# Two sums of weights per chunk by adding transfers, and a new route for turned blocks, in a hybrid transformer block on one core

## The chip, the cores and the metric

The kernel runs on one core of a Trainium2 chip. The metric is the device time of one launch in microseconds. The engines that matter are PE (matrix products, its weight loads shown as PEld), DVE and ACT (elementwise work), POOL and SP, which here do little but issue transfers: SP the loads of the weights, POOL the transfers of turned blocks. PE's clock has two levels, 2.4 and 1.2 GHz; the profile shows the granted one as a share of the higher.

## What is computed

One decoder layer on 256 tokens of 2048 values, in fp32. Cut to what matters:

```python
h = rmsnorm(x, attn_norm_w)
q, k, v, o, ig, fg, dq, dk, dv, gm, gd = split_in(h @ w_in)
hm = sigmoid(o) * head_rmsnorm(mlstm_chunkwise(q, k, v, ig, fg))
hd = head_rmsnorm(diff_attention(dq, dk, dv, lam)) * (1 - lam_init)
y  = sigmoid(gm) * (hm @ w_bm) + sigmoid(gd) * (hd @ w_bd)
x  = x + y @ w_out                                   # product wo
h  = rmsnorm(x, ffn_norm_w)
x  = x + (silu(h @ w_gate) * (h @ w_up)) @ w_down    # products fgu, fd; inner width 5632
return rmsnorm(x, final_norm_w)
```

## The kernel before

**Products.** Every weight is read from DRAM by SP in pieces of 1 MB (tiles `wr_...`, four buffers) and split into a high part (`wh`, a copy on ACT, L337) and a low part (`wl`, a subtraction on DVE, L341), so that three fp32r matmuls (L180, L181, L182: high by high, low by high, high by low) give the accuracy of fp32. The split of half a piece is a unit. It is made four units before PE uses it, into five buffers, so the copy of a unit waits until PE is through with the unit five before.

**Pairs.** The feed-forward part is a row of products: `fgu0` to `fgu3`, `fd00`, `fd02`, `fgu4` to `fgu7`, `fd10`, `fd12`, `fgu8` to `fgu10`, `fd20`, `fd22`, and `fd23`. All but the last two are pairs (16 of them), each of two blocks of 512 columns over four chunks of 512 rows (three in `fd20`). A pair takes one chunk by a scheme of seven products in place of eight (table SEVEN), in which some operands are sums: sums of blocks of x (made once per chunk by `add_up`, L160 to L164), and sums of weights, four per pair, each an addition in place on DVE (L329). The first chunk's seven units are dealt evenly among the plain units of the others. At a pair's end eight differences and sums on DVE (L416, tiles `q`) take its results from PSUM; for `fgu` an ACT Silu (L1123) and a DVE multiply (L1125) of each token half then make a block `g` of the inner layer. This happens while PE is already in the next pair.

**Turned blocks.** PE wants the left operand with its features in the partitions. A block of 256 tokens by 512 features gets there in one of three ways. `turn_task` has DVE turn it in squares of 32 (two transposes, L261), sends it to DRAM (one transfer from POOL's queue, L266), reads it back in another order (four, L271), and copies it into a high and a low part (L284 and L285, or with a scale L288 to L290); between the steps stand waits counted in ticks of the program's order, 4 and 10, one tick being six matmuls, so the place of a step in each engine's queue is fixed when the program is written. `turn_short_task` does it with 16 transposes of DVE (L230) and no DRAM. `transpose_task` uses eight transposes on PE (L193). The sets TURN and SHORT say which block takes which way. The blocks are y0 to y3 (input of `wo`), x1_0 to x1_3 (input of `fgu`; the last is `x1last`), g (input of `fd`; the last is `glast`), and some before. Lanes (`side.push("tr", ...)`) hold tasks that run one after the other: a block in a lane starts when the one ahead of it is through.

**Order.** Every engine executes its instructions in the order in which this program wrote them; an instruction that waits holds up all behind it on its engine.

Of the kernel before, what the change touches and what calls it, by code (L numbers as in the profile page):

```python
# [50 lines left out]
def hybrid_block(ctx, tc, x, attn_norm_w, w_in, conv_w, conv_b, b_igate, b_fgate, mlstm_norm_w,  # L51
# [266 lines left out]
    class Op:


        def __init__(self, pair, chunk, raw, half, add, uses, frees):
            self.pair, self.chunk, self.raw, self.half, self.add = pair, chunk, raw, half, add
            self.uses, self.frees, self.added, self.parts = uses, frees, False, None

        def sum_up(self):

            if self.add and not self.added:
                o, x = (feed.raw[g][:, 2 * h:2 * h + 2] for g, h in ((self.raw, self.half), self.add))
                nc.vector.tensor_tensor(out=o, in0=o, in1=x, op=ALU.add)  # L329
            self.added = True  # L330
# [990 lines left out]
```

## Time and profile before

| | |
|---|---|
| time, median of 3 runs | 1784.65 us (1783.57 to 1785.12) |
| the profiled execution | 1783.87 us, of which the span is 1781.8 us |
| mean granted clock of PE in it | 0.988 |
| PE / PEld / DVE / ACT / POOL busy | 97 / 80 / 71 / 52 / 5 % |
| DMA traffic | 362.52 MB, mean 203 GB/s |
| units split in pairs, `fgu` / `fd` | 209 / 91 |
| additions of weights on DVE (L329) | 64 of 1.22 us |

Busy is the time in which an engine executed something. A row of the timeline gives start and length in microseconds, engine, line, operation, output and inputs, and in brackets how long the engine was idle before it and which engine's instruction ended that. A table of waits sums these idle times by what waited and by what was waited for. Matmuls overlap in the pipeline: one lasts 0.39 us by its row and the next starts 0.23 us after it at the full clock; at half the clock the rows show 0.63 and 0.43 us.

### The profile page before, as it was taken

To read this page: it belongs to the slowest core of one execution; us is meant where nothing else is said; L and a number is where in the kernel's file an instruction comes from. 1 tells how busy PE (TensorE), PEld (TensorE's weight loads), DVE (VectorE), ACT (ScalarE), POOL (GpSimd) and SP (SyncE) were. 2 spreads that over 40 slices of the span, in tenths; PEclk is the share of its full clock that TensorE was granted. 3 is DMA by queue.
4 is the path that set the end of the run, shared out by engine and by line. 5 is a ranking of instruction groups with operands and counts; after the bars stand their busy time and mean duration, and the time that the engine had idled before them with its cause. 6 is when DMAs were issued, how large, how long until landed. Compare 5 with 4: busy or idle time off the path is not lost.

```text
span 1781.8 us, 20497 instructions
## 1 busy us (share of the span) xinstructions
PE 1735.7 (97%) x7769; PEld 1431.4 (80%) x7769; DVE 1272.4 (71%) x1692; ACT 921.1 (52%) x1189; POOL 86.0 (5%) x176
## 2 busy tenths in 40 slices
PE   9999999999999999999998988999999999999987
PEld 7888888888888888888887866788788787788766
DVE  6776876655456667665565666888788888788886
ACT  7555655654345555565443544555444555445543
POOL 1000000000001000100001000000000000000000
PEclk9999999999999999999999988999999999999999
DMA  9656566665677766766675745676566666566643
GB/s 305 198 167 185 167 200 177 190 230 200 189 217 216 215 203 189 210 191 211 230 243 195 227 144 171 202 243 223 188 205 219 206 235 229 179 205 226 219 171 116
DMA packets 179619, 362.52 MB, mean 203 GB/s; under 512 B 9904, under 2 KB 11584, under 8 KB 179520
## 3 DMA queue, kind: packets, MB, share of 16 engines
q1 hardware_dynamic: 169744, 330.78, 57.8%
q0 software_dynamic: 9744, 30.42, 5.7%
q8 instruction: 61, 1.00, 0.2%
q14 instruction: 38, 0.31, 0.0%
q10 hardware_dynamic: 32, 0.01, 0.0%
HBM read 343.88 MB, written 17.30 MB: 203 GB/s over the span
## 4 chain that ended last, share of the span: by engine, by line
PE 91%; DVE 4%; DMA 2%; issue 2%; ACT 2%; POOL 0%; SPq 0%; ACTq 0%; DVEq 0%; POOLq 0%
PE acc_fgu_P L181 7%; PE acc_fgu_P L180 7%; PE acc_fgu_P L182 7%; PE acc_fd_P L180 4%; PE acc_fd_P L182 4%; PE acc_fd_P L181 4%; PE acc_mo L180 2%; PE acc_mv L180 2%; PE acc_gm L180 2%; PE acc_dk L180 2%; PE acc_dq L180 2%; PE acc_gd L180 2%; PE acc_dv L182 2%; PE acc_dv L180 2%; PE acc_gd L182 2%; PE acc_mo L182 2%
## 5 line engine op out<-in xcount | busy, mean ns | idle before, releaser
L341 DVE TENSOR_TENSOR wl_fgu<-wr_fgu,wh_fgu 128x1024 fp32r<-128x1024 f32 x209 | 252.5, 1221 | 78.1 <-ACT wh_fgu L337 73.6
L337 ACT CAST wh_fgu<-wr_fgu 128x1024 fp32r<-128x1024 f32 x209 | 214.9, 1050 | 180.3 <-PE acc_fgu_P L182 107.6
L180 PE MATMUL acc_fgu_P<-wh_fgu,x1Th 128*128 128x512 f32 x594 | 234.0, 394 | 15.4 <-ACT x1Th L289 13.3
L181 PE MATMUL acc_fgu_P<-wl_fgu,x1Th 128*128 128x512 f32 x594 | 234.0, 394 | 4.1 <-DVE wl_fgu L341 4.1
L182 PE MATMUL acc_fgu_P<-wh_fgu,x1Tl 128*128 128x512 f32 x594 | 233.4, 393 | 0.0
L180 PEld LDWEIGHTS acc_fgu_P<-wh_fgu,x1Th 128*128 128x128 f32 x594 | 113.0, 190 | 40.3 <-ACT x1Th L289 14.1
L337 ACT CAST wh_fd<-wr_fd 128x1024 fp32r<-128x1024 f32 x91 | 94.0, 1050 | 91.2 <-PE acc_fd_P L182 67.4
L341 DVE TENSOR_TENSOR wl_fd<-wr_fd,wh_fd 128x1024 fp32r<-128x1024 f32 x91 | 110.2, 1222 | 38.9 <-ACT wh_fd L337 37.4
L181 PEld LDWEIGHTS acc_fgu_P<-wl_fgu,x1Th 128*128 128x128 f32 x594 | 112.9, 190 | 28.8 <-DVE wl_fgu L341 5.3
L182 PEld LDWEIGHTS acc_fgu_P<-wh_fgu,x1Tl 128*128 128x128 f32 x594 | 113.0, 190 | 23.8 <-DVE x1Tl L290 0.5
L266 POOL DMA_DIRECT2D across<-turned x29 | 16.4, 565 | 1421.5 <-DVE turned L261 1421.5
L271 POOL DMA_DIRECT2D across<-across x116 | 63.2, 552 | 144.2 <-DMA across<-turned 62.3
L485 DVE TENSOR_TENSOR wl_bm<-wr_bm,wh_bm 128x1024 fp32r<-128x1024 f32 x32 | 39.2, 1225 | 40.5 <-ACT wh_bm L484 40.5
L485 DVE TENSOR_TENSOR wl_dv<-wr_dv,wh_dv 128x1024 fp32r<-128x1024 f32 x32 | 39.2, 1224 | 37.0 <-ACT wh_dv L484 37.0
L485 DVE TENSOR_TENSOR wl_bd<-wr_bd,wh_bd 128x1024 fp32r<-128x1024 f32 x32 | 39.2, 1225 | 34.1 <-ACT wh_bd L484 34.1
L485 DVE TENSOR_TENSOR wl_wo<-wr_wo,wh_wo 128x1024 fp32r<-128x1024 f32 x32 | 38.9, 1222 | 33.2 <-ACT wh_wo L484 33.2
L485 DVE TENSOR_TENSOR wl_dk<-wr_dk,wh_dk 128x1024 fp32r<-128x1024 f32 x32 | 39.2, 1224 | 28.7 <-ACT wh_dk L484 28.7
L485 DVE TENSOR_TENSOR wl_gm<-wr_gm,wh_gm 128x1024 fp32r<-128x1024 f32 x32 | 39.1, 1224 | 27.9 <-ACT wh_gm L484 27.7
L485 DVE TENSOR_TENSOR wl_dq<-wr_dq,wh_dq 128x1024 fp32r<-128x1024 f32 x32 | 39.1, 1222 | 27.4 <-ACT wh_dq L484 27.3
L485 DVE TENSOR_TENSOR wl_gd<-wr_gd,wh_gd 128x1024 fp32r<-128x1024 f32 x32 | 39.1, 1223 | 26.9 <-ACT wh_gd L484 26.9
L484 ACT CAST wh_bd<-wr_bd 128x1024 fp32r<-128x1024 f32 x32 | 33.7, 1054 | 47.2 <-PE acc_bd L182 40.5
L484 ACT CAST wh_bm<-wr_bm 128x1024 fp32r<-128x1024 f32 x32 | 33.7, 1054 | 46.7 <-PE acc_bm L182 39.9
(430 smaller groups left out, 4635.9 us busy)
## 6 DMA issues: line engine op xcount, KB each, us to landing
wr_fgu<-in_w_ffn_gate_dram SPq DMA_DIRECT2D x44, 1024.0 KB, 5.2
wr_fgu<-in_w_ffn_up_dram SPq DMA_DIRECT2D x44, 1024.0 KB, 5.1
wr_fd<-in_w_ffn_down_dram SPq DMA_DIRECT2D x44, 1024.0 KB, 5.1
wr_mo<-in_w_in_dram SPq DMA_DIRECT2D x16, 1024.0 KB, 5.4
wr_mv<-in_w_in_dram SPq DMA_DIRECT2D x16, 1024.0 KB, 5.4
wr_gm<-in_w_in_dram SPq DMA_DIRECT2D x16, 1024.0 KB, 5.7
wr_bm<-in_w_branch_m_dram SPq DMA_DIRECT2D x16, 1024.0 KB, 5.1
wr_dq<-in_w_in_dram SPq DMA_DIRECT2D x16, 1024.0 KB, 5.4
```

What stands on the lines that cost most here:

```text
L180: nc.tensor.matmul(o, lhsT=a[0], rhs=b[0], start=first, stop=False)
L181: nc.tensor.matmul(o, lhsT=a[0], rhs=b[1], start=False, stop=False)
L182: nc.tensor.matmul(o, lhsT=a[1], rhs=b[0], start=False, stop=last)
L266: nc.gpsimd.dma_start(out=d.rearrange("a f b n -> (a f) (b n)"), in_=y.rearrange("p b k t s -> p (b k t s)"))
L271: nc.gpsimd.dma_start(out=t[32 * b:32 * b + 32].rearrange("p a u s -> p a (u s)"), in_=d[:, :, b].rearrange("a f n -> f a n"))
L337: nc.scalar.copy(out=hi, in_=r)
L341: nc.vector.tensor_tensor(out=lo, in0=r, in1=hi.bitcast(F32), op=ALU.subtract)
L484: nc.scalar.copy(out=hi[:, i:i + step], in_=r)
L485: nc.vector.tensor_tensor(out=lo[:, i:i + step], in0=r, in1=hi[:, i:i + step].bitcast(F32), op=ALU.subtract)
```

## The change

Four edits. (1) The table SEVEN gets a new order of units (P3, P2, P1, P4 to P7), and each unit a list of the sums that are formed after its split. Two, both after P2's split, stay additions on DVE; the other two, after P1's and P4's split, become transfers from SBUF to SBUF that add to their destination, issued from POOL's queue, 512 KB each. (2) `side.across` starts a turned block at once when its kind is in TURN and not in SHORT, in place of putting it in a lane. (3) SHORT holds `x1last` in place of `glast`; `glast`, which is in neither set then, goes through PE. (4) The Silu and the multiply that make `g` are written one tick later.

```diff
-SHORT = {"glast"}
+SHORT = {"x1last"}
...
+        def across(self, lane, kind, *rest):
+
+            gen = across_task(kind, *rest)
+            if kind in TURN and kind not in SHORT:
+                self.spawn(gen)
+            else:
+                self.push(lane, gen)
...
-    SEVEN = (("P3", (0, 1), None, (0, 1)), ("P1", (0, 0), None, (0, 0)), ("P2", (1, 0), None, "d"),
-             ("P4", (1, 0), (1, 1), "a"), ("P5", (1, 1), (0, 1), "b"), ("P6", (0, 1), (1, 0), "c"),
-             ("P7", (0, 0), (0, 1), (1, 0)))
+    VEC, DMA = "vector", "transfer"
+    SEVEN = (("P3", (0, 1), (0, 1), ()),
+             ("P2", (1, 0), "d", ((VEC, (1, 0), (1, 1)), (VEC, (1, 1), (0, 1)))),
+             ("P1", (0, 0), (0, 0), ((DMA, (0, 1), (1, 0)),)),
+             ("P4", (1, 0), "a", ((DMA, (0, 0), (0, 1)),)),
+             ("P5", (1, 1), "b", ()), ("P6", (0, 1), "c", ()), ("P7", (0, 0), (1, 0), ()))
...
-            self.sum_up()
...
-            nxt = feed.units[feed.nsplit + 1:feed.nsplit + 2]
-            if nxt and isinstance(nxt[0], Op):
-                nxt[0].sum_up()
             nc.vector.tensor_tensor(out=lo, in0=r, in1=hi.bitcast(F32), op=ALU.subtract)
+            for how, *terms in self.sums:
+                o, x = (feed.raw[g][:, 2 * h:2 * h + 2] for g, h in terms)
+                if how == VEC:
+                    nc.vector.tensor_tensor(out=o, in0=o, in1=x, op=ALU.add)
+                else:
+                    nc.gpsimd.dma_start(out=o, in_=x, accum_op=ALU.add)
...
-            side.push("tr", across_task("y" if c < 3 else "ylast", s, yT, c, None, 2 if c < 3 else 4))
+            side.across("tr", "y" if c < 3 else "ylast", s, yT, c, None, 2 if c < 3 else 4)
...
-            side.push("tr", across_task("x1" if c < 3 else "x1last", t, x1T, c, ffn_col, 2 if c < 3 else 4))
+            side.across("tr", "x1" if c < 3 else "x1last", t, x1T, c, ffn_col, 2 if c < 3 else 4)
...
                 t, c, q = got
+                yield
                 if c == 0:
                     nc.scalar.activation(out=g[:, t], in_=q, func=AF.Silu, scale=r2(t))
...
-            side.push("tr", across_task("g" if i < 2 or len(gT.hi) > 3 else "glast", g, gT, i, None, 4))
+            side.across("tr", "g" if i < 2 or len(gT.hi) > 3 else "glast", g, gT, i, None, 4)
```

Line numbers of the kernel after are some eight to ten higher (L261 becomes L269, L329 becomes L346, L341 becomes L342, L1125 becomes L1135). POOL's queue gets 32 adding transfers, from `fgu0` to `fd20`; in a pair whose predecessor gave a block `g`, the second one stands between that block's way out and its way back.

How the instructions move, at three places. First DVE around the start of `wo`; `sgd_6954` is the block y2 before, made in `bd2`, `sgd_7105` is y3, made in `bd3`, and `turned` is a block's first transposes. Before, y2 is turned behind the instructions that make y3:

```order
L485 TENSOR_TENSOR wl_wo_7686<-wr_wo_7599,wh_wo_7685 128x1024
L285 TENSOR_TENSOR yTl_7682<-across,yTh_7681 128x512
L485 TENSOR_TENSOR wl_wo_7704<-wr_wo_7599,wh_wo_7703 128x1024
L1084 TENSOR_TENSOR sgd_7105<-acc_bd_0_7572,sgd_7105 128x512
L1085 TENSOR_TENSOR sgd_7105<-y_3395,sgd_7105 128x512
L1084 TENSOR_TENSOR sgd_7105<-acc_bd_1_7573,sgd_7105 128x512
L1085 TENSOR_TENSOR sgd_7105<-y_3395,sgd_7105 128x512
L485 TENSOR_TENSOR wl_wo_7730<-wr_wo_7633,wh_wo_7729 128x1024
L261 STREAM_TRANSPOSE turned<-sgd_6954 128x4x4x32 x2
```

In the change (y2 is `sgd_6959`):

```order
L1093 TENSOR_TENSOR sgd_6959<-acc_bd_0_7417,sgd_6959 128x512
L1094 TENSOR_TENSOR sgd_6959<-y_3244,sgd_6959 128x512
L1093 TENSOR_TENSOR sgd_6959<-acc_bd_1_7418,sgd_6959 128x512
L1094 TENSOR_TENSOR sgd_6959<-y_3244,sgd_6959 128x512
L494 TENSOR_TENSOR wl_bd_7580<-wr_bd_7484,wh_bd_7579 128x1024
L494 TENSOR_TENSOR wl_bd_7596<-wr_bd_7484,wh_bd_7595 128x1024
L269 STREAM_TRANSPOSE turned<-sgd_6959 128x4x4x32 x2
```

The transposes of y2 stand two splits behind the instructions that make it, in `bd3`'s splits, in place of after the first ones of `wo`.

Second, DVE at the start of `fgu0`; `x_3` is the last block of x1, `x_2` the one before. Before:

```order
L1097 TENSOR_TENSOR x_3_7725<-acc_wo_1_8223,x_3_7725 128x512
L341 TENSOR_TENSOR wl_fgu_8387<-wr_fgu_8249,wh_fgu_8386 128x1024
L261 STREAM_TRANSPOSE turned<-x_2_7570 128x4x4x32
L341 TENSOR_TENSOR wl_fgu_8408<-wr_fgu_8285,wh_fgu_8407 128x1024
L261 STREAM_TRANSPOSE turned<-x_2_7570 128x4x4x32
L341 TENSOR_TENSOR wl_fgu_8422<-wr_fgu_8337,wh_fgu_8421 128x1024
L341 TENSOR_TENSOR wl_fgu_8445<-wr_fgu_8411,wh_fgu_8444 128x1024
L329 TENSOR_TENSOR wr_fgu_8337<-wr_fgu_8337 128x1024
L341 TENSOR_TENSOR wl_fgu_8467<-wr_fgu_8411,wh_fgu_8466 128x1024
L341 TENSOR_TENSOR wl_fgu_8480<-wr_fgu_8337,wh_fgu_8479 128x1024
```

In the change:

```order
L1106 TENSOR_TENSOR x_3_7735<-acc_wo_1_8228,x_3_7735 128x512
L342 TENSOR_TENSOR wl_fgu_8397<-wr_fgu_8358,wh_fgu_8396 128x1024
L346 TENSOR_TENSOR wr_fgu_8358<-wr_fgu_8358 128x1024
L346 TENSOR_TENSOR wr_fgu_8358<-wr_fgu_8358,wr_fgu_8249 128x1024
L342 TENSOR_TENSOR wl_fgu_8418<-wr_fgu_8301,wh_fgu_8417 128x1024
L238 STREAM_TRANSPOSE turned<-x_3_7735 32x2x4x32 x4
L342 TENSOR_TENSOR wl_fgu_8436<-wr_fgu_8249,wh_fgu_8435 128x1024
L238 STREAM_TRANSPOSE turned<-x_3_7735 32x2x4x32 x4
L298 TENSOR_TENSOR x1Tl_8462<-scaled,x1Th_8461 128x512
L238 STREAM_TRANSPOSE turned<-x_3_7735 32x2x4x32 x4
L342 TENSOR_TENSOR wl_fgu_8473<-wr_fgu_8421,wh_fgu_8472 128x1024
L298 TENSOR_TENSOR x1Tl_8462<-scaled,x1Th_8461 128x512
```

The two long transposes of `x_2` are gone from here (they stand in `wo`), sixteen short ones of `x_3` have come in, as four times four rows, and two additions (L346) stand in a row behind one split.

Third, DVE at the end of `fgu1`, in `fgu2`'s first units; `wl_fgu_9027` before is the first unit's low part, `wl_fgu_9095` the fifth's, `wl_fgu_9118` the sixth's; the `q` are the results of `fgu1`. Before:

```order
L341 TENSOR_TENSOR wl_fgu_9047<-wr_fgu_8984,wh_fgu_9046 128x1024
L416 TENSOR_TENSOR q_8809<-acc_fgu_P_8765,q_8809 128x512
L341 TENSOR_TENSOR wl_fgu_9065<-wr_fgu_8954,wh_fgu_9064 128x1024
L341 TENSOR_TENSOR wl_fgu_9077<-wr_fgu_9008,wh_fgu_9076 128x1024
L416 TENSOR_TENSOR q_8811<-acc_fgu_P_8769,q_8811 128x512
L341 TENSOR_TENSOR wl_fgu_9095<-wr_fgu_8984,wh_fgu_9094 128x1024
L416 TENSOR_TENSOR q_8810<-acc_fgu_P_8825,q_8810 128x512
L1125 SCALAR_TENSOR_TENSOR g<-q_8810,rs_x_8523,g 128x512
L416 TENSOR_TENSOR q_8812<-acc_fgu_P_8829,q_8812 128x512
L1125 SCALAR_TENSOR_TENSOR g<-q_8812,rs_x_8523,g 128x512
L341 TENSOR_TENSOR wl_fgu_9118<-wr_fgu_9008,wh_fgu_9117 128x1024
```

In the change (the fifth unit is `wl_fgu_9101`, the sixth `wl_fgu_9124`):

```order
L425 TENSOR_TENSOR q_8816<-acc_fgu_P_8773,q_8816 128x512
L342 TENSOR_TENSOR wl_fgu_9071<-wr_fgu_8961,wh_fgu_9070 128x1024
L342 TENSOR_TENSOR wl_fgu_9083<-wr_fgu_9008,wh_fgu_9082 128x1024
L425 TENSOR_TENSOR q_8818<-acc_fgu_P_8777,q_8818 128x512
L342 TENSOR_TENSOR wl_fgu_9101<-wr_fgu_9074,wh_fgu_9100 128x1024
L346 TENSOR_TENSOR wr_fgu_9074<-wr_fgu_9074 128x1024
L346 TENSOR_TENSOR wr_fgu_9074<-wr_fgu_9074,wr_fgu_8990 128x1024
L425 TENSOR_TENSOR q_8817<-acc_fgu_P_8831,q_8817 128x512
L1135 SCALAR_TENSOR_TENSOR g<-q_8817,rs_x_8564,g 128x512
L425 TENSOR_TENSOR q_8819<-acc_fgu_P_8835,q_8819 128x512
L342 TENSOR_TENSOR wl_fgu_9124<-wr_fgu_9008,wh_fgu_9123 128x1024
L1135 SCALAR_TENSOR_TENSOR g<-q_8819,rs_x_8564,g 128x512
```

Two additions have come in between the fifth and the sixth split, and the second multiply that makes `g` has gone behind the sixth. The four sums of block `gT0` (L160 to L164 before), which stood ahead of the first unit's split, now stand some rows further up, between the second and the third `q` row.

## Rows read from the trace of the kernel before

**Rows 1.** Page, busy time of each engine: microseconds, share, instructions.

```profile
PE 1735.7 (97%) x7769; PEld 1431.4 (80%) x7769; DVE 1272.4 (71%) x1692; ACT 921.1 (52%) x1189; POOL 86.0 (5%) x176
```

**Rows 2.** Waits of PE: total microseconds, times, longest.

```profile
PE acc_fgu_P L180 <- ACT x1Th L289: 13.3, 2, 7.4
PE acc_wo L180 <- ACT yTh L284: 5.3, 1, 5.3
PE acc_fd_P L180 <- ACT gT2h L241: 5.2, 1, 5.2
PE acc_fgu_P L181 <- DVE wl_fgu L341: 4.1, 3, 1.4
```

**Rows 3.** Timeline, PE around `wo` chunk 2: start, duration; idle before, releaser.

```profile
951.13 0.79 PE L180 MATMUL acc_wo<-wh_wo,yTh 128*128 128x512 f32 x1 [5.34 <-ACT yTh L284]
...
955.01 0.40 PE L180 MATMUL acc_wo<-wh_wo,yTh 128*128 128x512 f32 x1
```

**Rows 4.** Timeline, DVE and ACT around `wo`, block y2.

```profile
938.25 1.30 DVE L261 STREAM_TRANSPOSE turned<-sgd 128x512 f32<-128x512 f32 x2
...
950.46 1.14 ACT L284 CAST yTh<-across 128x512 fp32r<-128x512 f32 x2 [3.59 <-DMA across<-across]
```

**Rows 5.** Timeline, PE at the start of `fgu0`.

```profile
1033.13 0.57 PE L180 MATMUL acc_fgu_P<-wh_fgu,x1Th 128*128 128x512 f32 x1 [2.14 <-DVE x L1097]
...
1055.82 0.79 PE L180 MATMUL acc_fgu_P<-wh_fgu,x1Th 128*128 128x512 f32 x1 [5.88 <-ACT x1Th L289]
...
1060.68 0.39 PE L182 MATMUL acc_fgu_P<-wh_fgu,x1Tl 128*128 128x512 f32 x1
```

**Rows 6.** Line L329, instructions of DVE: count, durations in ns.

```profile
L329 DVE TENSOR_TENSOR wr_fgu<-wr_fgu x22: 1211/1218/1221, 1044.0 to 1684.9; 128x1024 f32<-128x1024 f32 x22
```

**Rows 7.** Timeline, DVE, then PE, around the end of `fgu1`.

```profile
1131.97 1.23 DVE L164 TENSOR_TENSOR gT0sl<-sums,gT0sh 128x1024 fp32r<-128x1024 f32 x1 [1.12 <-ACT gT0sh L163]
...
1149.05 1.22 DVE L341 TENSOR_TENSOR wl_fgu<-wr_fgu,wh_fgu 128x1024 fp32r<-128x1024 f32 x1
...
1150.32 0.50 PE L181 MATMUL acc_fgu_P<-wl_fgu,x1Th 128*128 128x512 f32 x1 [1.36 <-DVE wl_fgu L341]
```

**Rows 8.** Timeline, DVE, then PE, behind the end of `fgu2`.

```profile
1187.92 0.68 DVE L416 TENSOR_TENSOR q<-acc_fgu_P,q 128x512 f32<-128x512 f32 x1
1188.64 0.75 DVE L1125 SCALAR_TENSOR_TENSOR g<-q,rs_x,g 128x512 f32<-128x512 f32 x1
1189.31 1.22 DVE L341 TENSOR_TENSOR wl_fgu<-wr_fgu,wh_fgu 128x1024 fp32r<-128x1024 f32 x1
...
1192.66 0.39 PE L181 MATMUL acc_fgu_P<-wl_fgu,x1Th 128*128 128x512 f32 x1
```

**Rows 9.** Timeline, POOL, then ACT, in `fd00`.

```profile
1243.00 1.10 POOL L271 DMA_DIRECT2D across<-across  x2 [2.37 <-issue]
...
1253.77 0.61 ACT L284 CAST gT0h<-across 128x512 fp32r<-128x512 f32 x1
```

**Rows 10.** Timeline, DVE, then PE, in `fd20`.

```profile
1707.00 0.75 DVE L1125 SCALAR_TENSOR_TENSOR g<-q,rs_x,g 128x512 f32<-128x512 f32 x1
1711.20 0.87 DVE L230 STREAM_TRANSPOSE turned<-g 32x256 f32<-32x256 f32 x2
...
1722.74 0.79 PE L180 MATMUL acc_fd_P<-wh_fd,gT2h 128*128 128x512 f32 x1 [5.24 <-ACT gT2h L241]
...
1726.30 0.39 PE L182 MATMUL acc_fd_P<-wh_fd,gT2l 128*128 128x512 f32 x1
```

**Rows 11.** Line L193, transposes on PE of one block in `wo`.

```profile
L193 PE MATMUL ps_tr<-ident,sgd x8: 270/272/273, 958.4 to 959.2; 128*128 128x128 f32 x8
```

**Rows 12.** Line L266: from issue to landing.

```profile
DMA to landing us min/median/max: 3.3/4.9/7.6
```

**Rows 13.** Page, DMA queues: packets, MB, share of 16 engines.

```profile
q0 software_dynamic: 9744, 30.42, 5.7%
```

**Rows 14.** Windows, the pair product `fgu3`.

```profile
1181.00:1223.00 42.00, 42.00 (x187) 34.78 (x186) 35.73 (x38) 22.09 (x25) 2.74 (x5) 1.00 0.67 225
```

More of the change, by code (lines that the diff above doesn't have):

```diff
@@ L311, in __init__ @@
             self.hooks, self.ahead, self.by_token, self.steps = {}, AHEAD, False, {}
-    SEVEN = (("P3", (0, 1), None, (0, 1)), ("P1", (0, 0), None, (0, 0)), ("P2", (1, 0), None, "d"),
-             ("P4", (1, 0), (1, 1), "a"), ("P5", (1, 1), (0, 1), "b"), ("P6", (0, 1), (1, 0), "c"),
-             ("P7", (0, 0), (0, 1), (1, 0)))
-    class Op:
[L321 to L330, printed above, removed]
+    VEC, DMA = "vector", "transfer"
[4 more added lines that the diff above has]
+             ("P5", (1, 1), "b", ()), ("P6", (0, 1), "c", ()), ("P7", (0, 0), (1, 0), ()))
+    class Op:
+        def __init__(self, pair, chunk, raw, half, uses, sums, frees):
+            self.pair, self.chunk, self.raw, self.half = pair, chunk, raw, half
+            self.uses, self.sums, self.frees, self.parts = uses, sums, frees, None
         def split(self):
-            self.sum_up()
             r = feed.raw[self.raw][:, 2 * self.half:2 * self.half + 2]
@@ L360, in plan @@
                 if ch in self.sums:
-                    for i, (bank_, (blk, h), add, x) in enumerate(SEVEN):
+                    for i, (bank_, (blk, h), x, sums) in enumerate(SEVEN):
                         frees = [(ch, 1)] if i == 5 else [(ch, 0)] if i == 6 else []
-                        sevens.append((ch, (ch, blk), h, add and ((ch, add[0]), add[1]), [(bank_, x)], frees))
+                        sums = [(how, *(((ch, b), h2) for b, h2 in terms)) for how, *terms in sums]
+                        sevens.append((ch, (ch, blk), h, [(bank_, x)], sums, frees))
                 else:
@@ L367, in plan @@
                             uses = [((("P1", "P7"), ("P2", "P8"))[blk][t], (t, h)) for t in range(TT)]
-                            plain.append((ch, (ch, blk), h, None, uses, [(ch, blk)] if h else []))
+                            plain.append((ch, (ch, blk), h, uses, [], [(ch, blk)] if h else []))
             order = sorted([((i + 0.5) / len(l), n, x) for n, l in enumerate((sevens, plain)) for i, x in enumerate(l)],
@@ L373, in plan @@
             self.ops = []
-            for ch, raw, h, add, uses, frees in order:
+            for ch, raw, h, uses, sums, frees in order:
                 if raw not in keys:
@@ L377, in plan @@
                     feed.groups.append((self, raw))
-                self.ops.append(Op(self, ch, keys[raw], h, add and (keys[add[0]], add[1]), uses,
-                                   [keys[f] for f in frees]))
+                self.ops.append((ch, raw, h, uses, sums, frees))
+            self.ops = [Op(self, ch, keys[raw], h, uses, [(how, *((keys[r], h2) for r, h2 in terms)) for how, *terms in sums],
+                           [keys[f] for f in frees]) for ch, raw, h, uses, sums, frees in self.ops]
             feed.units += self.ops
@@ L1061, in f @@
             qk[side_name] = dst
-            side.push("conv", across_task("d" + side_name, tok, dst, 0, rate=2))
+            side.across("conv", "d" + side_name, tok, dst, 0)
         return f
```

4 lines of the change are left out of this document (2 added, 2 removed).

## The prediction

> **What bounds the kernel now.** I read the busy times first: PE works 97% of the span, DVE 71% [rows 1]. With PE that full, only two things can shorten the time: fewer matmuls (the change leaves their number as it is, but for eight transposes) or fewer holes in PE. So the second view was the table of PE's waits. Its large entries are few [rows 2]: 13.3 us at two blocks of x1, 5.3 at a block of y, 5.2 at the last g, and 4.1 in three waits for a low part of weights. Third, I followed each into the timeline, where a hole costs more than its length. Behind the wait for y2, 5.34 us long, the matmuls from 951.13 to 955.01 are nine in 3.88 us [rows 3]; in a full stretch a matmul takes 42.00/187 = 0.225 us [rows 14], nine 2.03. The start at half clock costs 1.85 us more. So does the one behind x1's third block: eleven matmuls from 1055.82 to 1060.68 in 4.86 us in place of 2.48, 2.4 more [rows 5]. Fourth, the windows: in `fgu3` PE is busy without a break while DVE is busy 35.73 and ACT 22.09 of 42.00 us [rows 14]. There, work taken from DVE is worth nothing by itself. What decides is the work that stands in front of a low part that PE is about to need.
>
> **The change part by part.**
>
> *Block y2.* It is turned at 938.25, and ACT's copy waits at 950.46 for the last of its transfers [rows 4]: 12.2 us from the one to the other. In the new order its transposes stand two splits behind the instructions that make it, in `bd3`, about 24 us earlier by the place in the program. The copy is then ready long before. I take off 5.34 + 1.85 = **-7.2**; the bounds are 0 and -7.2, since nothing larger hangs on it.
>
> *Blocks 2 and 3 of x1.* Before: holes of 2.14, 5.88 and 7.41 us [rows 2, 5], 15.4 in all, with 2.4 us of half clock behind each of the two long ones and some 1.7 behind the short one (an estimate: it was shorter), so 21.9. The 2.14 waits for DVE's addition that frees a bank and stays, with its 1.7. Block 2 is turned in `wo`, so its hole goes. Block 3 no longer goes through DRAM but by sixteen transposes on DVE, 0.87/2 = 0.44 us each by the rows of `glast` [rows 10], 7.0 us, between splits and beside two additions of 1.22 [rows 6]. Following DVE's new order, the last transpose is through about 17.7 us into `fgu0`, and the copies of the turned block, on ACT, stand ahead of the copy of unit 8. PE reaches unit 8 after 78 matmuls, 17.6 us in. I put 2.7 us of new holes at units 8 to 10, and 0.8 of half clock. Before 21.9, after 2.14 + 1.7 + 2.7 + 0.8 = 7.4: **-14.5**. Bounds: -18 (no new holes) and -8 (the new ones are a whole DVE queue late, about as long as one old hole).
>
> *Ends of `fgu1`, `fgu5`, `fgu9`.* PE waits there 4.1 us in three waits [rows 2]: the sixth unit's low part starts at 1149.05 and lasts 1.22, and PE goes on at 1150.32 [rows 7]. In front of it DVE now has two additions more (2.44) and one multiply less (0.75): 1.7 us later. Besides, the sums of block g, whose last part starts at 1131.97 after 1.12 us of waiting and takes 1.23 [rows 7], now stand behind the first unit's split and not ahead of it; DVE makes up some of these 2.35 us in its pauses, and I take 1.3 of them. So +3.0 at each of three places, **+9**; from 1.7 to 4.1 each, 5 to 12.
>
> *The other seven ends of `fgu` products that give a turned g.* The sixth unit's part starts at 1189.31, ends at about 1190.5, and PE uses it at 1192.66 [rows 8]: 2.1 us to spare. The same 1.7 us fit, with 0.4 left: **0**. This is the cover that is nearly gone. Each microsecond beyond costs seven.
>
> *Blocks g in `fd00` and `fd10`.* Their turn starts some 3 us later (two additions, the split ahead of the second multiply), and the second adding transfer stands between the way out and the way back on POOL. Before, the last transfers back were issued by 1244.10 and ACT took the block at 1253.77 [rows 9]; the spread from issue to landing is wide [rows 12]. I take +1 each, **+2**; 0 to +12.
>
> *The last g.* Before 5.24 us, and eight matmuls from 1722.74 to 1726.30, 3.56 in place of 1.80, so 7.0 [rows 10]. PE would have used the block at 1717.5. In the new order the eight PE transposes stand 36 matmuls ahead of that use, at 1709.4. The second multiply ended at 1707.75 [rows 10] and now comes after two additions and one split more, 3.66, at 1711.4: a hole of 2.1, the transposes themselves 1.0 [rows 11], half clock 0.9. After 4.0, **-3.0**; from -6 to +1.
>
> *The adding transfers.* 32 additions, 39 us of DVE, become 32 transfers of 512 KB. The trace has no adding transfer. The nearest rows: a block's way out, also 512 KB, lands 3.3 to 7.6 us after issue [rows 12]; POOL's 30.42 MB took 5.7% of the sixteen engines' span [rows 13], 0.057 x 1781.8 / 30.42 = 3.3 us per MB, 1.75 per transfer. The first is needed by P6's copy some 15 us after issue, the second by P7's about as late. Landing in 3.3 to 7.6 they are hidden, and even twice that is borderline at most. In `fgu3` the DMA engines are busy 0.67 of 42 us [rows 14], 28.1 us; 2 x 1.75 makes it 31.6, and if reading the destination counts double, 35.1, still under 42. I take **0**, by the nearer row; the other end is below.
>
> The Trainium skill, "DMA: Bandwidth & Descriptors" (Issuing engines are not separate DMA queues), says that all issuing engines' transfers go through the same sixteen DMA engines and interleave; by that, the additions lengthen the landing of weights and don't run in a queue of their own. No run here shows an adding transfer beside loads; at the bounds above the sum would not change.
>
> **Sum.** -7.2 - 14.5 + 9 + 0 + 2 - 3.0 + 0 = -13.7. The profiled execution took 1783.87, 0.8 under the median of the runs. 1783.9 - 13.7 + 0.8 = 1771.0 us, 0.8% less.
>
> **Rivals.**
>
> *A: all holes close.* DVE loses 39 us in the pairs, and ACT's copies no longer wait for additions; the fifth unit's split could come early enough that the two additions fit ahead of the sixth. Then +9 turns to -4, +2 to 0, x1 gives 18 and the last g 6: -7.2 - 18 - 4 - 6 = -35, **1750**. For it: DVE has 6 us in 42 to spare [rows 14]. Against: order, not share, decides at a product's end, and both additions of a pair stand there.
>
> *B: nothing is left of it.* The seven other ends miss by 2 us each, since DVE comes 2.1 us later than I think: +14, and the sum is zero, **1784 to 1785**. For it: the cover is 0.4 us. Against: the sums of g, which make the three ends late, don't stand at these seven.
>
> *C: slower, by the DMA engines.* One mechanism, in all sixteen pairs: an adding transfer holds the engines far longer than a copy, since each element is read at both ends, added and written. The pair's 42.2 us leave 42.2 - 28.1 = 14 us, 7 per transfer; from there the loads set the pace. At 8 us each a pair is 2 us longer: +32, less the 13.7 saved, **1803**; at 8.5, 1819. For it: weight pieces at a pair's start have little time to spare, and one transfer would only have to take 4.6 times a copy's share. Against: in the copies' rows there is no sign of it.
>
> The Trainium skill, "SBUF — State Buffer" (Who interferes with whom), gives C a second way: a DVE instruction with two SBUF inputs contends with a GpSimd instruction that reads SBUF, and descriptors of GpSimd's transfers can starve under some DVE modes. The trace's row for POOL's issue, two in 1.10 us while DVE split weights [rows 9], doesn't show it.
>
> **How the numbers follow.** Two measurements of this kernel can be told apart from about 0.2%, 3.6 us. My forecast has 0.52, with a range of its own of 1760 to 1781 from the bounds of x1, the ends and g. A has 0.17, B 0.14, C 0.17 (with landings that are late in some pairs only among its milder cases, from 1788 up). Faster: the forecast and A, 0.69; same: most of B, 0.13; slower: C and a little of B, 0.18. The range from 1750 to 1795 leaves out half of A's tail and the worse part of C.
>
> **What will show it.** Right: in PE's waits yTh is gone; x1Th in `fgu0` is down to a few microseconds; wl_fgu has grown to about 13 us in three waits of some 4.4, with none at the other ends; a wait of the last g's transposes for DVE of about 2 us. DMA's share in a pair rises from 0.67 to between 0.75 and 0.85, and no copy of ACT waits for an adding transfer. Wrong: waits of wh or wl for loads or for adding transfers in every pair (C); waits for wl_fgu in ten places (B); none at all at the three ends (A).

## The result, and the profile after

The changed kernel took 1797.69 us (median of 3 runs, 1794.67 to 1798.67) against 1784.65 before: ratio 1.007, interval 1.0048 to 1.0093. It is slower by 13 us where 14 less were forecast, and outside the range. The profiled execution's span is 1795.9 us, 14.1 more than before.

The first view is the page: busy time of the engines, queues with packets, MB and share of the sixteen DMA engines, and the chain of work that ended last.

```profile
PE 1743.6 (97%) x7777; PEld 1433.2 (80%) x7777; DVE 1232.2 (69%) x1660; ACT 912.7 (51%) x1185; POOL 112.6 (6%) x203
...
q0 software_dynamic: 14016, 46.15, 10.7%
...
PE 75%; DVE 11%; DMA 8%; issue 3%; ACT 3%; SPq 0%; DVEq 0%; ACTq 0%
```

DVE did lose its 40 us [rows 1], and PE is as busy as before. But the software queue went from 5.7 to 10.7% of the DMA engines' time for 15.7 MB more [rows 13], and loads now stand in the chain with 8%. PE's waits, the view that answers to [rows 2]:

```profile
PE acc_fgu_P L189 <- DVE wl_fgu L342: 18.8, 14, 3.2
PE acc_fd_P L188 <- ACT gT1h L292: 4.9, 1, 4.9
PE acc_fd_P L189 <- DVE wl_fd L342: 4.9, 3, 2.1
PE acc_fd_P L188 <- ACT gT0h L292: 4.9, 1, 4.9
PE acc_fgu_P L188 <- ACT wh_fgu L341: 3.4, 4, 0.9
```

The long waits for yTh and x1Th are gone, as forecast. In their place stand waits for low parts of weights, 18.8 us in fourteen (13 in three were forecast), and 4.9 us each for a block g in `fd00` and `fd10`.

ACT, whose copies come ahead of the low parts, now waits for loads of weights in the pairs: 155.9 us in 38 waits, where before it was 4.7 in four. Two of the three rows:

```profile
ACT wh_fgu L341 <- DMA wr_fgu<-in_w_ffn_up_dram: 83.1, 18, 8.5
ACT wh_fd L341 <- DMA wr_fd<-in_w_ffn_down_dram: 39.7, 10, 9.2
```

That is the sign that the prediction gave for its rival C, in a good part of the pairs and not in every one. The adding transfers themselves are waited for by no copy.

To see where, I took the time from the first matmul of each product to that of the next, in all kernels. The table gives the difference to before, in us of the profiled execution (ends: `fgu2`, `fgu6`, `fgu10`, the pairs behind an `fgu` in which a block g gets its sums; the pairs not listed and `fd22`, `fd23` are within 0.1 of before except where "rest" says so; what lies ahead of `wo` is not in it, 0.9 us in g4, 0.6 in e3, at most 2.2, in f3). One of f2's four runs, 2089.9 us at a granted clock of 0.78, is left out of its median.

| kernel | median us | wo | fgu0 | ends | fgu3, fgu7 | fd00, fd10 | fd20 | rest |
|---|---|---|---|---|---|---|---|---|
| the change | 1797.7 | -9.2 | -16.5 | +18.1 | +5.2 | +17.6 | -1.1 | 0 |
| e1 no tick | 1791.0 | -9.2 | -16.5 | +17.9 | +1.2 | +11.2 | -2.1 | +1.7 |
| e2 all on DVE | 1782.2 | -9.2 | -14.3 | +12.0 | +1.5 | +8.8 | -0.8 | 0 |
| e3 old sums | 1751.2 | -9.2 | -16.4 | +0.8 | 0 | -1.3 | -6.9 | 0 |
| e4 sums alone | 1820.8 | +2.7 | +1.7 | +19.7 | +2.2 | +10.1 | 0 | +1.7 |
| e5 routes alone | 1752.4 | -9.3 | -16.5 | 0 | 0 | +3.2 | -6.2 | 0 |
| f1 units alone | 1752.6 | -9.2 | -16.5 | +0.8 | 0 | +1.8 | -6.9 | 0 |
| f2 row later | 1772.0 | -9.2 | -12.9 | +5.8 | +0.7 | +8.4 | -4.3 | 0 |
| f3 transfers later | 1814.3 | -9.2 | -14.0 | +15.1 | +9.8 | +25.8 | +1.9 | +1.4 |
| g1 idle adding | 1771.2 | -9.2 | -16.4 | +4.3 | +2.3 | +12.1 | -5.1 | 0 |
| g2 idle copies | 1754.7 | -9.2 | -16.5 | +1.1 | 0 | +0.1 | -5.8 | 0 |
| g3 last g on PE | 1747.2 | -9.2 | -16.5 | +0.8 | 0 | -4.4 | -6.9 | 0 |
| g4 DVE in fd | 1793.9 | -9.2 | -16.4 | +15.8 | +8.5 | +11.9 | -1.9 | 0 |

The change's row adds up to +14.1, its span's difference. Five ordinary pairs (`fgu1`, `fgu4`, `fgu5`, `fgu8`, `fgu9`) are the same to a tenth of a microsecond in the change: adding transfers and all, nothing is lost there.

At the ends, the place of [rows 7], the timeline of DVE and then PE in `fgu2` (start, duration, instruction, in brackets idle before and releaser) shows:

```profile
1122.47 1.23 DVE L342 TENSOR_TENSOR wl_fgu<-wr_fgu,wh_fgu 128x1024 fp32r<-128x1024 f32 x1 [1.73 <-ACT wh_fgu L341]
1123.73 1.23 DVE L346 TENSOR_TENSOR wr_fgu<-wr_fgu 128x1024 f32<-128x1024 f32 x1
1124.99 1.23 DVE L346 TENSOR_TENSOR wr_fgu<-wr_fgu,wr_fgu 128x1024 f32<-128x1024 f32 x1
1126.13 0.68 DVE L425 TENSOR_TENSOR q<-acc_fgu_P,q 128x512 f32<-128x512 f32 x1
1126.85 0.75 DVE L1135 SCALAR_TENSOR_TENSOR g<-q,rs_x,g 128x512 f32<-128x512 f32 x1
1127.52 0.68 DVE L425 TENSOR_TENSOR q<-acc_fgu_P,q 128x512 f32<-128x512 f32 x1
1128.12 1.22 DVE L342 TENSOR_TENSOR wl_fgu<-wr_fgu,wh_fgu 128x1024 fp32r<-128x1024 f32 x1
...
1129.39 0.80 PE L189 MATMUL acc_fgu_P<-wl_fgu,x1Th 128*128 128x512 f32 x1 [3.23 <-DVE wl_fgu L342]
```

The fifth unit's low part, two additions, three rows for g, the sixth's low part: PE waits 3.23 where it waited 1.36.

In `fd00`, the place of [rows 9], POOL, ACT and PE:

```profile
1224.51 0.91 POOL L348 DMA_DIRECT2D wr_fd<-wr_fd  x1
1228.58 2.23 POOL L279 DMA_DIRECT2D across<-across  x4 [3.17 <-DMA across<-turned]
...
1238.68 4.83 ACT L341 CAST wh_fd<-wr_fd 128x1024 fp32r<-128x1024 f32 x5 [9.20 <-DMA wr_fd<-in_w_ffn_down_dram]
1243.42 1.14 ACT L292 CAST gT0h<-across 128x512 fp32r<-128x512 f32 x2
...
1244.09 0.50 PE L188 MATMUL acc_fd_P<-wh_fd,gT0h 128*128 128x512 f32 x1 [4.88 <-ACT gT0h L292]
1244.42 0.54 PE L189 MATMUL acc_fd_P<-wl_fd,gT0h 128*128 128x512 f32 x1
1246.18 0.80 PE L190 MATMUL acc_fd_P<-wh_fd,gT0l 128*128 128x512 f32 x1 [1.22 <-DVE gT0l L293]
```

ACT stands 9.20 us for a load of weights, catches up on five copies, and only then takes the block. The load is in the chain of that stretch as one piece from 1224.78, its issue, on:

```profile
1224.78 13.80 DMA wr_fd<-in_w_ffn_down_dram
```

In the kernel before, these loads of 1 MB landed in 5.1 us by the median. The view of the DMA queues over the stretch 1218 to 1246 says what was beside it (queue: packets, MB, share of the sixteen engines; issues: count, size, median us to landing):

```profile
q0 software_dynamic: 624, 2.10, 34.0%
...
wr_fd<-wr_fd POOLq DMA_DIRECT2D x2, 512.0 KB, 8.1
across<-turned POOLq DMA_DIRECT2D x1, 512.0 KB, 4.1
across<-across POOLq DMA_DIRECT2D x4, 128.0 KB, 7.9
```

So two adding transfers (the second from 1224.51 to 1235.12), the block's way out and back, and six loads meet there. Of the loads the two behind the slow one were issued at 1230.00 and 1231.14, while it was still on its way, and landed after 11.27 and 12.71 us. Of the slow load's sixteen landing signals fourteen had come 8.61 us after its issue; the last two came at 13.27 and 13.80. The block itself landed at 1238.56, at the same moment as the load; ACT did five copies, 4.8 us, ahead of it, about as long as PE's hole of 4.88.

All over the feed-forward part, 22 of 132 such loads took more than 10 us to land in the change, 1 before (counted in the traces).

### The profile page after: what moved, and what is told of

Same layout as the page of the kernel before. It is cut to its first block, busy times and chain, and to the rows that moved or that the text cites. A ratio compares the mean times of both kernels' runs of the same rounds, so it can differ in the third digit from the quotient of the medians.

```text
span 1795.9 us, 20627 instructions
## 1 busy us (share of the span) xinstructions
PE 1743.6 (97%) x7777; PEld 1433.2 (80%) x7777; DVE 1232.2 (69%) x1660; ACT 912.7 (51%) x1185; POOL 112.6 (6%) x203
## 3 DMA queue, kind: packets, MB, share of 16 engines
q0 software_dynamic: 14016, 46.15, 10.7%
## 4 chain that ended last, share of the span: by engine, by line
PE 75%; DVE 11%; DMA 8%; issue 3%; ACT 3%; SPq 0%; DVEq 0%; ACTq 0%
DMA wr_fgu<-in_w_ffn_up_dram 5%; DVE wl_fgu L342 4%; PE acc_fgu_P L189 3%; PE acc_fgu_P L190 3%; PE acc_fgu_P L188 3%; PE acc_fd_P L190 3%; PE acc_fd_P L188 3%; PE acc_fd_P L189 3%; DMA wr_fd<-in_w_ffn_down_dram 2%; DVE q L425 2%; ACT wh_fgu L341 2%; PE acc_mv L188 2%; PE acc_mo L188 2%; PE acc_gm L188 2%; PE acc_dq L188 2%
## 5 line engine op out<-in xcount | busy, mean ns | idle before, releaser
L342 DVE TENSOR_TENSOR wl_fgu<-wr_fgu,wh_fgu 128x1024 fp32r<-128x1024 f32 x209 | 247.9, 1220 | 121.3 <-ACT wh_fgu L341 119.8
L341 ACT CAST wh_fgu<-wr_fgu 128x1024 fp32r<-128x1024 f32 x209 | 211.6, 1049 | 197.8 <-DMA wr_fgu<-in_w_ffn_up_dram 83.1
L189 PE MATMUL acc_fgu_P<-wl_fgu,x1Th 128*128 128x512 f32 x594 | 234.7, 395 | 18.8 <-DVE wl_fgu L342 18.8
L342 DVE TENSOR_TENSOR wl_fd<-wr_fd,wh_fd 128x1024 fp32r<-128x1024 f32 x91 | 108.5, 1221 | 64.5 <-ACT wh_fd L341 64.3
L341 ACT CAST wh_fd<-wr_fd 128x1024 fp32r<-128x1024 f32 x91 | 93.5, 1049 | 99.8 <-PE acc_fd_P L190 59.3
L494 DVE TENSOR_TENSOR wl_mv<-wr_mv,wh_mv 128x1024 fp32r<-128x1024 f32 x32 | 38.9, 1222 | 23.0 <-ACT wh_mv L493 22.7
```

Of the source, the lines that this page charges most:

```text
L189: nc.tensor.matmul(o, lhsT=a[0], rhs=b[1], start=False, stop=False)
L341: nc.scalar.copy(out=hi, in_=r)
L494: nc.vector.tensor_tensor(out=lo[:, i:i + step], in0=r, in1=hi[:, i:i + step].bitcast(F32), op=ALU.subtract)
```

## The experiments

Two theories stood at first: P, the place of instructions in DVE's and ACT's queues at a product's end, and D, the time that adding transfers take on the DMA engines. All kernels are built from the changed one or from before.

**e1**, the change without the extra tick:

```diff
                 t, c, q = got
-                yield
```

> The changed kernel without the extra tick ahead of the Silu and of the multiply that make g; everything else as changed. Changed: 1797.7 us; against before, its pairs lose 7.4, 4.7 and 6.0 us in fgu2, fgu6, fgu10 (the ones behind a g with sums), 9.1 and 8.5 in fd00 and fd10, 4.5 in fgu7, and the ordinary pairs nothing. Theory P (place: the later g pushes the copies and sums of the turned block into the pair's end, among the q rows and ahead of the next low parts): fgu2, fgu6, fgu10 lose at most 3 each, fgu7 nothing, fd00 and fd10 at most 4, so about 1773 to 1780. Theory D (the adding transfers hold the DMA engines, and loads and turned blocks land late): the fd pairs still lose 8 each and the time is 1788 or more.

1790.99 us, ratio to before 1.0029 (1.0018 to 1.0040). The tick costs some 6.7 us together with the new sums, in `fd00`, `fd10` and `fgu7`; the ends lose as much as with it. The two `fd` pairs lose 11.2 together, where D had 8 each. P with the tick as its cause falls.

**e2**, all four sums on DVE at the places of the change:

```diff
-    VEC, DMA = "vector", "transfer"
+    VEC, DMA = "vector", "vector"
```

> The changed kernel with its two adding transfers per chunk made additions on DVE, at the same places in the order of units. Theory D: no load lands later than about 8 us after issue in fd00 and fd10, these pairs lose 2 to 3 us in place of 9, and the time is about 1784, although DVE does 39 us more. Theory P: the same copies stand at the same ends with more on DVE in front of them; the fd pairs lose as before or more, and the time is 1797 to 1806.

1782.21 us, 0.9982 (0.9971 to 0.9992). 39 us more on DVE, and 15.5 us less in all: the transfers cost more than they take from DVE. One load of 132 takes more than 10 us. But 12.0 us at the ends and 8.8 in the `fd` pairs stay, so D is a part of it, and P, without the tick as its cause, another.

**e3**, edits 2 to 4 on the kernel before, that is the old table SEVEN and `sum_up`:

```diff
-    VEC, DMA = "vector", "transfer"
...
+            self.sum_up()
...
+            if nxt and isinstance(nxt[0], Op):
+                nxt[0].sum_up()
```

> Before with the new routes of turned blocks and the extra tick, but the old order of units and all four additions on DVE, one ahead of each split that uses it. Theory P with the tick as its cause: the three ends with sums and fgu7 still lose, 3 to 5 us each, the fd pairs 4 or more: about 1775 to 1785. Theory D, or theory P with the two additions in a row as its cause: nothing is lost at any end (under 1 us each), the 26 us won at wo and fgu0 stay, about 1759 to 1764.

1751.22 us, 0.9812 (0.9791 to 0.9832), below what was expected. All losses but 0.8 us at the ends are gone, and the last g gives 6.9 us in place of 1.1. Both the tick and the new routes are free by themselves; the first edit, the sums, is what costs, 46 us of it.

**e4**, edit 1 alone, the complement:

```diff
-SHORT = {"x1last"}
+SHORT = {"glast"}
...
-                yield
...
-            side.across("tr", ...)
+            side.push("tr", across_task(...))
```

> Before with only the new order of units and the two adding transfers per chunk; routes, lanes and ticks of the turned blocks as before. Theory D: fd00 and fd10 lose 6 to 9 us each, from a load that lands over 10 us after issue: about 1800. Theory P with the tick as its cause: the three ends with sums lose 1 to 2 us for the two additions, everything else stays: about 1786 to 1790.

1820.76 us, 1.0198 (1.0166 to 1.0229): worse than either theory gave. The ends lose 19.7 with the old routes, and `wo` and `fgu0` another 2.7 and 1.7, where y2 and x1's blocks still went through DRAM (PE waits 7.1 us for yTh in place of 5.3, and 15.8 for x1Th in place of 13.3). The sums cost 35 us without the new routes, 46 with them.

The next four split edit 1. It has three parts: the order of units (P2 ahead of P1), the place of the additions, and the transfers.

**f1**, e3 with the order of units alone:

```diff
-    SEVEN = (("P3", (0, 1), None, (0, 1)), ("P1", (0, 0), None, (0, 0)), ("P2", (1, 0), None, "d"),
+    SEVEN = (("P3", (0, 1), None, (0, 1)), ("P2", (1, 0), None, "d"), ("P1", (0, 0), None, (0, 0)),
```

> The kernel with new routes, tick and the additions of before (e3, 1751.2 us) with one more edit: the units P1 and P2 change places, as in the change; all four additions stay on DVE, each ahead of the split that uses it. Theory U (the new order of units costs, since P2's block of weights is then needed two units earlier and ACT waits for its load): ACT waits for loads at the fifth unit and the three ends with sums and the fd pairs lose 3 to 5 us each, about 1770 to 1782. Theory R (the two additions in a row between the fifth and the sixth split cost): nothing changes, 1750 to 1755.

1752.57 us, 0.9816 (0.9801 to 0.9830): the order of units costs nothing. f1 and e2 have the same units and the same four additions on DVE, and differ in their place by 29.6 us. All four stand elsewhere in e2, two of them in a row, so the 29.6 is the price of the early places together and not of the row alone.

**f2**, the old order of units, additions in a row behind P2's split, two units later than in e2:

```diff
+             ("P1", (0, 0), (0, 0), ()),
+             ("P2", (1, 0), "d", ((VEC, (1, 0), (1, 1)), (VEC, (1, 1), (0, 1)))),
+             ("P4", (1, 0), "a", ((VEC, (0, 1), (1, 0)),)),
+             ("P5", (1, 1), "b", ((VEC, (0, 0), (0, 1)),)),
```

> The changed kernel with all four additions on DVE, in the old order of units: the first two in a row behind P2's split, which is then the seventh unit and not the fifth, the third behind P4's, the fourth behind P5's. Against e2 (1782.2 us) the row of two has gone behind the sixth unit's split and behind the q rows. Theory R: the three ends, fgu7 and the first hole of the fd pairs are gone, 1751 to 1758. If a row of two costs wherever it stands: 1770 or more. Theory U: 1751 to 1755 as well, so f1 tells U from R.

1771.97 us, 0.9926 (0.9910 to 0.9943): in the expectation's words a row of two costs wherever it stands, 1770 or more. The ends lose half of what they did in e2, the `fd` pairs as much, and `fgu0` and `fd20` give back 3.6 and 2.6 us less than in f1. DVE's timeline in `fd00`, from the second multiply that makes g to the block's transposes:

```profile
1215.02 0.75 DVE L1135 SCALAR_TENSOR_TENSOR g<-q,rs_x,g 128x512 f32<-128x512 f32 x1
1215.68 1.22 DVE L342 TENSOR_TENSOR wl_fd<-wr_fd,wh_fd 128x1024 fp32r<-128x1024 f32 x1
1216.93 1.23 DVE L346 TENSOR_TENSOR wr_fd<-wr_fd 128x1024 f32<-128x1024 f32 x1
1218.19 1.22 DVE L346 TENSOR_TENSOR wr_fd<-wr_fd,wr_fd 128x1024 f32<-128x1024 f32 x1
1219.34 1.22 DVE L342 TENSOR_TENSOR wl_fd<-wr_fd,wh_fd 128x1024 fp32r<-128x1024 f32 x1
1220.47 1.30 DVE L269 STREAM_TRANSPOSE turned<-g 128x512 f32<-128x512 f32 x2
```

In f1 the same stretch is:

```profile
1207.60 0.75 DVE L1134 SCALAR_TENSOR_TENSOR g<-q,rs_x,g 128x512 f32<-128x512 f32 x1
1210.53 1.30 DVE L269 STREAM_TRANSPOSE turned<-g 128x512 f32<-128x512 f32 x2
```

From g to its transposes it is 5.45 us in f2 and 2.93 in f1: the row of additions has gone in front of the turned block. But these 2.5 us aren't yet what PE waits for, 3.8 us in place of 1.7. In f1 the block landed at 1221.73 and ACT took it 6.8 us later, when its copies of units were through:

```profile
1228.58 1.14 ACT L292 CAST gT0h<-across 128x512 fp32r<-128x512 f32 x2
```

In f2 it landed at 1234.33, and ACT took it only at 1237.67, behind copies that waited for a load:

```profile
1235.77 1.99 ACT L341 CAST wh_fd<-wr_fd 128x1024 fp32r<-128x1024 f32 x2 [3.80 <-DMA wr_fd<-in_w_ffn_down_dram]
1237.67 1.13 ACT L292 CAST gT0h<-across 128x512 fp32r<-128x512 f32 x2
```

The chain that ended last shows why that load was late: it was issued when DVE's low parts, late themselves, gave back its buffer.

```profile
1225.15 2.28 DVE wl_fd L342 x2
1227.44 8.23 DMA wr_fd<-in_w_ffn_down_dram
```

That is 23.6 us into the pair, against 20.3 in f1; in e2's `fd00` it is 24.4, and ACT takes the block behind such a load too. So the early additions cost in two ways: a low part that PE needs stands behind them at a product's end, and low parts that come late give buffers back late, so loads are issued late and ACT comes late to the block. The third and the fourth addition are early in f2 as well; no run parts the row of two from earliness alone.

**f3**, transfers in the old order of units, one addition at a time:

```diff
+             ("P2", (1, 0), "d", ((VEC, (1, 0), (1, 1)),)),
+             ("P4", (1, 0), "a", ((VEC, (1, 1), (0, 1)), (DMA, (0, 1), (1, 0)))),
+             ("P5", (1, 1), "b", ((DMA, (0, 0), (0, 1)),)),
```

> Two adding transfers per chunk as in the change, but in the old order of units and one addition at a time: the first addition on DVE behind P2's split, the second behind P4's with the first transfer, the second transfer behind P5's, some 9 us ahead of their use. Theory R alone (the place of DVE's additions is all that costs): no worse than e3, 1747 to 1752. Theory D beside it (the transfers' time on the DMA engines delays loads and turned blocks in fd00 and fd10): these two pairs lose 3 to 5 us each against e3, and P6 or P7 may wait for a transfer, 1757 to 1775.

1814.30 us, 1.0157 (1.0140 to 1.0174), above both ranges. With less time between issue and use, ACT waits for the transfers themselves:

```profile
ACT wh_fgu L341 <- DMA wr_fgu<-wr_fgu: 44.7, 19, 4.6
```

They land in 8.1 us by the median here, 10.3 at most. So a transfer needs an early place, as it has in the change, and early places are what costs on DVE: the two faults are tied.

**e5**, the routes alone, e3 without the tick:

```diff
                 t, c, q = got
-                yield
```

> Before with the new routes of turned blocks alone (no extra tick, additions as before). If the extra tick is worth something, this is 2 us or more above e3 (1751.2 us); if the routes carry all, 1749 to 1753.

1752.42 us, 0.9818 (0.9803 to 0.9833): the routes carry all of it, the tick nothing that can be told.

**g1** and **g2**, f1 with 32 transfers more whose result nobody uses, adding in g1, copying in g2 (no `accum_op`):

```diff
+            if self.bank in ("P1", "P4"):
+                if not spare:
+                    spare.append(scratch())
+                nc.gpsimd.dma_start(out=spare[0], in_=r, accum_op=ALU.add)
```

> f1 (new routes, units P3, P2, P1, all four additions on DVE just ahead of their use; 1752.6 us) plus 32 adding transfers of 512 KB whose result nobody uses: behind P1's and P4's split, from the unit's weights into one spare tile. It asks what the transfers cost by themselves, with no addition moved. Theory D (they hold the DMA engines about twice as long as a copy, so loads and a turned block's transfers land late where both meet): fd00 and fd10 lose 3 to 5 us each against f1, the other pairs 0 to 1, about 1758 to 1765; the software queue's share rises by some 5% of the span. If the transfers are free and only the additions' place costs: 1751 to 1755.

> As g1, but the 32 transfers copy and don't add. Theory D: half the time on the engines (share up by 2 to 3%), fd00 and fd10 lose 0 to 2 us each, 1752 to 1757. If it is POOL's queue (the place between the way out and the way back) and not the engines' time that costs, the same as g1 within 2 us.

g1: 1771.18 us, 0.9913 (0.9896 to 0.9930); g2: 1754.67, 0.9825 (0.9810 to 0.9839). Same queue, same places, same bytes: copies cost 2 us, additions 18.6. Their place in POOL's queue alone is therefore not the cause. (In g1 ten loads of the pairs also wait, 9.1 us together, for such a transfer to finish reading their buffer, in g2 none; in the change no load waits for an adding transfer.) The software queue of the whole run, on f1's page:

```profile
q0 software_dynamic: 9408, 29.37, 5.5%
```

on g1's:

```profile
q0 software_dynamic: 14016, 46.15, 11.4%
```

and on g2's:

```profile
q0 software_dynamic: 14016, 46.15, 8.5%
```

The landing of the block's way back in 28 us of `fd00`, from the view of the DMA queues, first g1:

```profile
across<-across POOLq DMA_DIRECT2D x4, 128.0 KB, 7.7
```

then g2:

```profile
across<-across POOLq DMA_DIRECT2D x4, 128.0 KB, 5.2
```

For 16.8 MB that is (11.4% of 1769.5 less 5.5% of 1752.0) = 105 us of all sixteen engines adding, 3.3 per transfer, and (8.5% of 1751.3 less the same) = 52 copying, 1.6 per transfer. I had expected 1758 to 1765 for g1; D was right in kind and too small, 18.6 us in place of 5 to 12.

The later way back is not what PE waits for. In g1's `fd00` the block landed at 1230.15, and ACT took it 5 us later, behind copies that waited for a load:

```profile
1233.32 1.99 ACT L353 CAST wh_fd<-wr_fd 128x1024 fp32r<-128x1024 f32 x2 [2.60 <-DMA wr_fd<-in_w_ffn_down_dram]
1235.22 1.14 ACT L292 CAST gT0h<-across 128x512 fp32r<-128x512 f32 x2
```

Of the 132 loads of the feed-forward part 14 took more than 10 us in g1, 2 in g2 and none in f1.

**g4**, the change with DVE additions in `fd00` and `fd10` alone:

```diff
-                if how == VEC:
+                if how == VEC or self.pair.name in ("fd00", "fd10"):
```

> The changed kernel (1797.7 us) with its adding transfers replaced by DVE additions in fd00 and fd10 alone, the other 14 pairs as changed. Theory D (the transfers cost where a turned block is needed within the same pair): fd00 and fd10 fall from 9.1 and 8.5 us lost to about 4.5, as in e2, the rest stays: 1787 to 1791. If the transfers cost a bit everywhere by POOL's queue or ACT's waits: 1793 to 1798.

1793.88 us, 1.0046 (1.0031 to 1.0061). The two pairs fall from 17.6 to 11.9 (`fd00` loses 7.4 and `fd10` 4.5, where some 4.5 each were expected), but `fgu3` loses 3.3 more than in the change. It lies in the range for a cost everywhere: the transfers also hurt where a block passes in `fgu` pairs, as g1 shows for `fgu7` and the ends. In `fd00`, with no adding transfer in the pair, a load still took 12.7 us, beside loads issued 1.1 us apart and the block: a late load doesn't need an adding transfer beside it.

**g3**, a version that beats both: e3 with the last g of every part through PE.

```diff
-            side.across("tr", "g" if i < 2 or len(gT.hi) > 3 else "glast", g, gT, i, None, 4)
+            side.across("tr", "g" if i < len(gT.hi) - 1 else "glast", g, gT, i, None, 4)
```

> e3 (1751.2 us) with the last g of the first two parts too through PE's eight transposes in place of DRAM, as the change does with the very last. In e3 fd00 and fd10 have holes of 1.7 and 0.6 us with half clock behind them, 2.7 and 3.4 us over an ordinary pair. Expected: holes gone, 1 us of transposes and up to 1 us of waiting for g each, so 1747 to 1751; if the transposes stand too early in PE's row and wait for DVE's multiply, 1751 to 1755.

1747.24 us, 0.9783 (0.9768 to 0.9797). In PE's waits nothing is left of g in `fd00` and `fd10`; low parts of weights come first:

```profile
PE acc_fgu_P L189 <- DVE wl_fgu L349: 5.9, 8, 1.1
```


## Why the prediction was wrong

*Blocks y2 and x1: right.* Forecast -7.2 and -14.5, measured -9.2 and -16.5 [rows 3 to 5]. About 1.2 of the surplus in `wo` is the wait for the bank, 0.97 us in place of 2.14; the new holes in `fgu0` are 0.87, 0.77 and 1.14, the 2.7 that was forecast, with no half clock behind them (granted clock 1.00 from 1024 to 1070), where 2.5 us had been put behind these and the wait for the bank.

*The three ends: right in mechanism, half in size.* Forecast +9, measured +18.1. The hole behind the sixth unit's part is 3.23 and not 4.4, but earlier units miss as well (0.32, 0.86 and 0.76 in `fgu2`): the sums of g, for which I had put 1.3 us, hold ACT ahead of the second unit's copy:

```profile
1110.81 1.05 ACT L171 CAST gT0sh<-sums 128x1024 fp32r<-128x1024 f32 x1 [4.80 <-DVE sums L168]
1111.77 1.05 ACT L341 CAST wh_fgu<-wr_fgu 128x1024 fp32r<-128x1024 f32 x1
```

(ACT's timeline in the change.) In `fgu2` the granted clock is 0.93 (1.00 in `fgu6`), and the pair loses 7.4 us where `fgu6` loses 4.7. The 6.1 us beyond e2's 12.0 are the transfers and this clock together, in one profile; some of the earlier holes are e2's too (one of 0.58 in `fgu2`).

*The cover at the seven other ends: held at three, not at four.* In `fgu1`, `fgu5` and `fgu9` nothing is lost. In `fgu3`, `fgu7`, `fd00` and `fd10` another block g is copied at the same end, which [rows 8] don't show, and the 0.4 us left were gone: 0.4, 2.56, 2.06 and 2.08 us of hole. I had taken one end for all seven. Loads have a part in it: in `fgu3` and `fgu7` ACT waited 2.58 and 4.99 us for a load shortly ahead of that block's copy.

*Blocks g in the fd pairs: the largest miss.* Forecast +2, measured +17.6. The sum counted the later start of the block and looked at the transfers of POOL's queue alone; that a load issued beside them would take 13.8 us, with ACT's copies and the block behind it in ACT's queue, was not in it.

*The last g: smaller than forecast.* Forecast -3.0, measured -1.1. The transposes wait 1.12 us for DVE's multiply where 2.1 was forecast, but two holes ahead of them, 0.94 for a copy of weights and 0.75 for a low part, were not foreseen, and the granted clock in `fd20` is 0.91. With the additions just ahead of their use (f1) it gives 6.9.

*The adding transfers at 0: the failed step, with the place of the early additions.* The sum went by the row of a copy, 1.75 us per transfer, with the double as a bound at which "the sum would not change", since a pair's 42 us still had room. The double is what g1 measured, 3.3. And the room over a whole pair was the wrong test. `fgu4` and `fgu5` have that room and lose nothing, at a DMA share of 0.73 and 0.83 (0.75 to 0.85 was forecast, 0.60 and 0.68 was it before),

```profile
1304.80:1346.90 42.10, 42.10 (x187) 34.87 (x186) 30.65 (x32) 20.84 (x21) 1.74 (x2) 1.00 0.73 225
1347.00:1389.00 42.00, 42.00 (x187) 34.79 (x186) 30.80 (x36) 19.19 (x22) 4.56 (x7) 1.00 0.83 250
```

(duration, then PE, PEld, DVE, ACT and POOL busy, granted clock, DMA share, GB/s), while in the 28 us of `fd00` in which two adding transfers, the block's five transfers and six loads meet, the software queue alone took 34% of the engines' time. There the landing times of single loads, and when they were issued, decide, not the mean. The transfers cost 15.5 us in the change (over e2) and 18.6 by themselves (g1 over f1), where the sum has 0.

The Trainium skill's sentence that all issuing engines share the sixteen DMA engines ("DMA: Bandwidth & Descriptors", Issuing engines are not separate DMA queues) agrees with g1: loads that SP issues land late beside POOL's adding transfers, 14 of 132 in more than 10 us, against 2 beside copies and none beside neither. The second way to rival C, DVE against GpSimd, which the prediction took from the Trainium skill's page "SBUF — State Buffer" (Who interferes with whom), is not seen in g2: its copies go through the same queue beside the same DVE and cost 2 us, and POOL's issue takes 0.54 to 0.57 us there.

*The rivals.* C named a right cause, more engine time per added byte, but with all pairs paced by their loads; no ordinary pair is longer, and the time near C's is a coincidence of sums. B's late ends came at four places of seven. A was wrong for the change: DVE's 39 us gave nothing back, and it is e3, with all four additions on DVE, that closes most of the holes.

The additions' place is the other half of the failed step, and the larger: e2 less f1 is 29.6 us, with no transfer in either. For the new sums together the prediction had +11 (9 at the ends, 2 in the `fd` pairs, 0 for the transfers); the change less e3 is 46. I had read order rows at one end and priced two additions there. They stand in front of the sixth unit, of the multiply, of the transposes of every block and of the last g (`fd20`: -0.8 in e2, -6.9 in f1), and by late low parts they delay the loads behind.

What stays open: g4's +3.3 in `fgu3`, seen in one profile; how much of the loss in the change is transfers and how much is early additions at each single place, since only the sums are separated; how much of the additions' 29.6 us is the row of two; whether a block's way back is late behind an adding transfer by POOL's one queue or by the engines' time; and why two of sixteen parts of the 13.8 us load came 5 us after the others.

## What to carry to other kernels

Work that was taken from DVE, which was not the bound here, gained nothing, but its new place cost: the four additions just ahead of their use were free, the same four earlier, two of them in a row, cost 30 us. Before giving work to the DMA engines, look at the stretch where loads and a transfer that something waits for already meet, not at the mean share, and count an adding transfer at twice a copy, as measured here. An instruction's place also decides when a buffer comes free and so when a load is issued. When a change has several edits, run them apart: three of four edits here made 1.9% (e3, 1751.2 us), and the fourth hid it.
